# Wide one-hots, unscaled expert queries and fewer float32 pairs in a two-layer decoder trunk with a product-key FFN

## Chip, cores and metric

The kernel runs on one core of one Trainium2 chip. The metric is device time in microseconds of the whole program, the median over runs. The engines are named as in the profile: PE (TensorE, matrix multiplication), DVE (VectorE), ACT (ScalarE), POOL (GpSimd) and SP (SyncE, which issues the transfers). Every tensor in SBUF has 128 partitions.

## The reference, cut to what matters

There are two layers over 256 tokens of width 1024. A layer mixes tokens by three branches (sliding-window attention, a gated convolution and a recurrence), then applies the product-key FFN, then a gated projection of a side input. The change touches the FFN alone:

```
def peer(xn, w_q, sub_keys, u, v):          # t = 256 tokens, 8 heads, 128 x 128 keys, top 16
    q  = (xt @ w_q).reshape(t, 8, 2, 128)
    sc = einsum('thpc,pnc->thpn', q, sub_keys)
    top_s, top_i = top_k(sc, 16)
    cand = top_s[:, :, 0, :, None] + top_s[:, :, 1, None, :]
    best_s, best_c = top_k(cand.reshape(t, 8, 256), 16)
    i1, i2 = (take_along_axis(top_i[:, :, a], ...) for a in (0, 1))   # best_c // 16 and best_c % 16
    expert, gate = i1 * 128 + i2, softmax(best_s)
    act = gelu(einsum('cd,chkd->chk', x, u[expert]))
    return einsum('chk,chkd->cd', gate * act, v[expert])
```

Here xn = RMSNorm(h), that is h times a weight per column, times r2, one positive factor per token.

## The kernel before, in words

**All experts, densely.** The kernel doesn't gather rows of u and v. It multiplies the tokens by all 16,384 rows of u, weights the result with a matrix of gates that is zero where an expert wasn't chosen, and multiplies by all rows of v. Rows come in 64 *pairs* of 2 x 128 experts. `u_pass(i)` (line 642) loads one pair of u (1 MB), multiplies, and applies Gelu into a tile `acts` that holds four pairs. `v_pass(i)` (660) reads gates, multiplies them in, and accumulates into four PSUM banks. The loop at line 700 runs i from 0 to NPAIR + RUN_AHEAD: u_pass(i), and v_pass(i - RUN_AHEAD) once i has reached RUN_AHEAD.

**Two forms of a multiplication.** The result has to be nearly of float32 accuracy. Either PE multiplies in float32, or each operand is cut into a high and a low part (type float32r) and three products are summed (`mm3`, 184). For the second form `split` (153) makes the parts of 1024 columns of weights: ACT casts to the high part, DVE subtracts to get the low one. Each part has three buffers. In u_pass, pairs below WHOLE = 20 are multiplied in float32 straight from the loaded tile with the scaled tokens `x2w`; the others by mm3 with the parts of the scaled tokens `x2`. All other weights come through `Stream` (170), which splits the next 1024 columns as they are needed.

**Queries and routing.** For each of the eight heads `pair` multiplies the unscaled tokens `x2g` by the weights w_peer_q (two splits per head), DVE multiplies the result by r2 into `q` (507), and `scores` (485) multiplies by the keys and finds the top 16 of each half by DVE's instructions for maxima and their positions. `route(b)` (517) forms the candidates of 128 tokens, finds the best 16 and turns their positions into the two expert numbers e1 and e2; `soften(b)` (571) makes the gates gt with ACT's Exp; `turn(b)` (585) transposes e1, e2 and gt on PE and spreads each value over four neighbouring float16 elements (`eT`, and `g2` with high and low part).

**The matrix of gates.** For 8 tokens at a time, `hot(tg)` (601) compares eT with 0 to 127 and so makes one-hots on DVE: `o1` of e1 in a buffer of its own, `og` of e2, and two products of o1 with the parts of g2. `place(tg)` (620) has PE multiply these (16 multiplications of 128 x 128) into PSUM, ACT copies them to a stage, and every second group is written to HBM (`gd`). v_pass reads gd back. og is in pool `xp` with four buffers, two of which hold x2 during the FFN.

**What sets the order.** The framework fixes ahead of time an order for each engine's queue: of what is ready, what was written down first goes first, and instructions under `high_priority(offset=200)` (splits, loads and the queries' line 507) rank as if they had been written 200 instructions earlier. Each engine runs its queue in order. Tiles of one tag share that tag's buffers; route and turn share `rcode` (one buffer) and soften's gt shares one with route. By hand are written: scores of the last head and route(0) in pair 0; soften(0) ahead of pair 7; turn(0) and route(1) ahead of pair 8; soften(1) ahead of pair 13, turn(1) ahead of pair 14; and `matrix` (689), called three times in each pair: from pair G_START = 10 on, each call places the group before last and starts the one-hots of the next. There are 32 groups, so the last placing falls into pair 21. Line 713 demands that all of it was written down before v begins.

Of the kernel before, what the change touches and what calls it, by code (L numbers as in the profile page):

```python
# [7 lines left out]
F32 = mybir.dt.float32  # L8
F32R = mybir.dt.float32r
F16 = mybir.dt.float16  # L10
I32 = mybir.dt.int32
U32 = mybir.dt.uint32
AF = mybir.ActivationFunctionType
OP = mybir.AluOpType
# [4 lines left out]
P = 128  # L19
# [4 lines left out]
TOPK = 16  # L24
NPAIR = 64
G_START = 10
RUN_AHEAD = 24
WHOLE = 20
TG = 8
REP = 4  # L30
GPAD = 16
# [28 lines left out]
def plan():  # L60

    out = []

    def cols(name, c0, n):
        for c in range(n):
            for k in range(KT):
                out.append((name, k * P, c0 + c * P))

    cols("w_in", C_K, 2)
    cols("q", 0, 8)  # L70
    for k in range(KT):
        for m in range(2):
            out.append(("w_in", k * P, C_V + m * P))
    for j in range(0, KT, 2):
        cols("w_in", C_CX + j * P, 2)
        cols("w_in", C_CC + j * P, 2)
        cols("w_in", C_CB + j * P, 2)
    for j in range(0, KT, 2):
        cols("w_in", C_RX + j * P, 2)
        cols("w_in", C_RY + j * P, 2)  # L80
    for n in range(3):
        for j in range(0, KT, 2):
            cols("w_in", C_G + n * 1024 + j * P, 2)
            if n == 0:
                for name in ("w_rgate", "w_igate"):
                    for jo in range(2):
                        for ki in range(2):
                            out.append((name, (j // 2, ki * P), jo * P))
            cols("b%d" % n, j * P, 2)
    cols("w_out", 0, 8)  # L90
    cols("w_peer_q", 0, 16)
    for c in range(8):
        for k in range(2):
            out.append(("w_ple_proj", k * P, c * P))
    cols("w_ple_gate", 0, 8)
    return out
# [3 lines left out]
def trunk_kernel(ctx: ExitStack, tc: tile.TileContext, xT, pT, vecs, wmix, wu, wv, outT, dbg=None, layers=NL):  # L100
    nc = tc.nc
# [4 lines left out]
    xp = pool("xp", 4)  # L106
# [3 lines left out]
    small = pool("small", 2)  # L110
# [9 lines left out]
    def aux_bank(name, shape=(P, 2, T)):  # L120
        return psum.tile(list(shape), F32, name=name, tag="aux", bufs=2)
# [16 lines left out]
    ident = cst.tile([P, P], F32, name="ident")  # L138
# [11 lines left out]
    nc.gpsimd.memset(eps, EPS)  # L150


    def split(src, name, cuts=1):

        with tc.high_priority(offset=AHEAD):
            hi = parts.tile([P, 1024], F32R, name=name + "h", tag="hi")
            lo = parts.tile([P, 1024], F32R, name=name + "l", tag="lo")
            for c in range(cuts):
                s = slice(c * 1024 // cuts, (c + 1) * 1024 // cuts)
                nc.scalar.copy(hi[:, s], src[:, s])  # L160
                nc.vector.tensor_sub(lo[:, s], src[:, s], hi[:, s].bitcast(F32))
        return hi, lo

    def load(src, name):
# [5 lines left out]
    class Stream:  # L170
        def __init__(self, l):
            self.l, self.n, self.raw, self.cur = l, 0, None, None

        def next(self, w=1):
            if self.n % 16 == 0:
                self.raw = load(wmix[self.l, self.n // 16], "w%d_%d" % (self.l, self.n // 16)) if self.l or self.n else first
            if self.n % 8 == 0:
                o = self.n % 16 * P
                self.cur = split(self.raw[:, o : o + 1024], "w%d_%d" % (self.l, self.n // 8), 1 if self.l or self.n else 2)
            o = self.n % 8 * P  # L180
            self.n += w
            return self.cur[0][:, o : o + w * P], self.cur[1][:, o : o + w * P]
# [85 lines left out]
    def rb(rstd):  # L268
        return rstd[:, None, :].to_broadcast([P, 2, T])
# [12 lines left out]
    def t2(name, shape, dt=F32):  # L282
        return work.tile(list(shape), dt, name=name, tag="t2", bufs=3)
# [5 lines left out]
    def layer(l):  # L289
# [15 lines left out]
        for kt in range(KT):  # L305
            w = st.next(2)
# [196 lines left out]
        for hd in range(HEADS):  # L503
            ps = pair(st, x2g, L + "pq%d" % hd)
            q = work.tile([P, 2, T], F32, name=L + "pqs%d" % hd, tag="w2a")
            with tc.high_priority(offset=AHEAD):
                nc.vector.tensor_mul(q, ps, rb(r2))
            if last:
                scores(*last)
            last = (hd, q)  # L510
            if 2 <= hd < 6:
                x2 = scaled(V + V_FFN, r2, L + "n2", (2 * hd - 4, 2 * hd - 3), x2, x2w)
# [58 lines left out]
        def soften(b):  # L571
            n = L + "r%d" % b
            e1, e2, best = chosen[b]

            gt = small.tile([P, HEADS, TOPK], F32, name=n + "gt", tag="rsf", bufs=1)
            nc.vector.tensor_sub(gt, best, best[:, :, 0:1].to_broadcast([P, HEADS, TOPK]))
            nc.scalar.activation(gt, gt, AF.Exp)
            gs = small.tile([P, HEADS], F32, name=n + "gs", tag="rgs", bufs=1)
            nc.vector.tensor_reduce(gs, gt, axis=AX.X, op=OP.add)
            nc.vector.reciprocal(gs, gs)  # L580
            nc.vector.tensor_mul(gt, gt, gs[:, :, None].to_broadcast([P, HEADS, TOPK]))
            chosen[b] = (e1, e2, gt)


        def turn(b):
            n = L + "r%d" % b

            pt = aux_bank(n + "pt", (P, 3, P))
            for i, a in enumerate(chosen[b]):
                nc.tensor.transpose(pt[:, i, :], a.rearrange("p h k -> p (h k)"), ident)  # L590
            eT = small.tile([P, 2, P, REP], F16, name=n + "eT", tag="eT", bufs=2)
            nc.vector.tensor_copy(eT, pt[:, 0:2, :, None].to_broadcast([P, 2, P, REP]))
            g2 = small.tile([P, 2, P, REP], F16, name=n + "g2", tag="g2", bufs=2)
            rest = small.tile([P, P], F32, name=n + "rest", tag="rcode", bufs=1)
            nc.vector.tensor_scalar(rest, pt[:, 2, :], GS, None, op0=OP.mult)
            rep = rest[:, :, None].to_broadcast([P, P, REP])
            nc.vector.tensor_copy(g2[:, 0], rep)
            nc.vector.tensor_sub(g2[:, 1], rep, g2[:, 0])
            routed.append((eT, g2))

        def hot(tg):

            eT, g2 = routed[tg // (P // TG)]
            m = L + "t%d" % tg
            o = tg % (P // TG) * TG

            S = [P, TG, P // REP, REP]
            bc = lambda a: a[:, o : o + TG, None, :].to_broadcast(S)
            index = iota_i.rearrange("p (i r) -> p i r", r=REP)[:, None, :, :].to_broadcast(S)
            o1 = t2(m + "o1", S, F16)  # L610
            og = xp.tile([P, 3] + S[1:], F16, name=m + "og", tag="x")
            nc.vector.tensor_tensor(o1, index, bc(eT[:, 0, :]), op=OP.is_equal)
            nc.vector.tensor_tensor(og[:, 2], index, bc(eT[:, 1, :]), op=OP.is_equal)
            for i in range(2):
                nc.vector.tensor_mul(og[:, i], o1, bc(g2[:, i]))
            return og

        stage = [None]
# [195 lines left out]
```

## Time and profile before

| | |
|---|---|
| median of 3 runs | 2480.21 us (2479.56 to 2480.83) |
| the profiled execution's own time | 2482.27 us |
| its span on the core | 2480.6 us |
| granted TensorE clock, mean of the span | 0.991 |
| PE / DVE / ACT / POOL busy | 2443.6 / 1696.8 / 1228.9 / 28.8 us |
| moved by DMA | 485.92 MB, mean 196 GB/s |

The span is that of one profiled execution, and the time of that execution is 1.67 us longer. Busy times of different engines overlap, so they aren't added up. A granted clock of 1.00 is TensorE's full 2.4 GHz.

### The profile page before, as it was taken

Reading aid. Unit: us, or ns where it says so; the run is one execution under the profiler, and the core shown is the slowest. Engines: PE = TensorE matmul, PEld = TensorE weight load, DVE = VectorE, ACT = ScalarE, POOL = GpSimd, SP = SyncE. Lnnn points to the kernel's source line nnn. Section 1 sums busy time; section 2 is a strip of 40 time slices with the busy share of each in tenths; the row PEclk is TensorE's granted clock in tenths of the full one; section 3 lists DMA queues with packets and bytes.
Section 4 is the critical chain, followed back from the end, with each engine's and each line's share of the span. In section 5 each row is a group of like instructions: output and inputs, shape, how many; then the busy total and the mean of one; then the engine's idle time right before and its main releaser. Section 6 shows DMA issues by size and latency. Waiting matters only on the chain.

```text
span 2480.6 us, 40695 instructions
## 1 busy us (share of the span) xinstructions
PE 2443.6 (99%) x16696; PEld 2243.2 (90%) x16696; DVE 1696.8 (68%) x3020; ACT 1228.9 (50%) x1605; POOL 28.8 (1%) x44
## 2 busy tenths in 40 slices
PE   8999999999999999999999999999999999999997
PEld 7899999889999999988879999998899999999886
DVE  7666869987655555567776668699865555555666
ACT  5555544167444444444654564532664444444445
POOL 0000100000000000000000010000000000000000
PEclk9999999999999999999999999999999999999998
DMA  5255444468755656575424445533785565665752
GB/s 194 102 187 181 172 176 152 145 232 310 246 206 206 223 204 218 206 254 197 170 109 146 179 169 187 187 136 143 275 308 212 204 221 204 211 213 206 265 191 86
DMA packets 129452, 485.92 MB, mean 196 GB/s; under 512 B 7536, under 2 KB 73200, under 8 KB 74864
## 3 DMA queue, kind: packets, MB, share of 16 engines
q1 hardware_dynamic: 128976, 482.90, 54.8%
q8 instruction: 131, 2.15, 0.3%
q10 hardware_dynamic: 288, 0.41, 0.1%
q14 instruction: 57, 0.47, 0.1%
HBM read 448.67 MB, written 34.60 MB: 195 GB/s over the span
## 4 chain that ended last, share of the span: by engine, by line
PE 97%; DVE 2%; ACT 1%; DMA 1%; issue 0%; SPq 0%; DVEq 0%; ACTq 0%
PE L0acc L681 14%; PE L1acc L681 14%; PE L0ua L655 6%; PE L1ua L655 5%; PE L0ua L185 3%; PE L1ua L185 3%; PE L1ua L187 3%; PE L0ua L187 3%; PE L1ua L186 3%; PE L0ua L186 3%; PE L1mg L187 1%; PE L0mg L187 1%; PE L0mg L186 1%; PE L1mg L186 1%; PE L1mg L185 1%; PE L0mg L185 1%
## 5 line engine op out<-in xcount | busy, mean ns | idle before, releaser
L655 PE MATMUL L0ua<-L0n2w,L0u 128*128 128x256 f32 x640 | 145.1, 382 | 0.0
L655 PE MATMUL L1ua<-L1n2w,L1u 128*128 128x256 f32 x640 | 145.1, 382 | 0.0
L655 PEld LDWEIGHTS L1ua<-L1n2w,L1u 128*128 128x128 f32 x640 | 119.0, 190 | 14.8
L655 PEld LDWEIGHTS L0ua<-L0n2w,L0u 128*128 128x128 f32 x640 | 119.0, 190 | 14.8
L658 ACT ACTIVATE L1act<-L1ua 128x512 f32<-128x512 f32 x64 | 38.0, 594 | 46.4 <-PE L1ua L655 46.4
L658 ACT ACTIVATE L0act<-L0ua 128x512 f32<-128x512 f32 x64 | 38.0, 594 | 46.4 <-PE L0ua L655 46.3
L669 DVE TENSOR_TENSOR L0wt<-L0act,L0gr 128x256 f32<-128x256 f32 x128 | 53.4, 421 | 2.7 <-DMA L0gr<-L0gd 0.7
L669 DVE TENSOR_TENSOR L1wt<-L1act,L1gr 128x256 f32<-128x256 f32 x128 | 53.4, 421 | 2.5 <-DMA L1gr<-L1gd 0.5
L439 DVE RECIPROCAL L1ru<-L1ru 128x256 f32<-128x256 f32 x8 | 14.0, 1746 | 0.1
L439 DVE RECIPROCAL L0ru<-L0ru 128x256 f32<-128x256 f32 x8 | 13.9, 1743 | 0.1
L380 POOL MEMSET L1pc<- 128x4 f32 x4 | 0.4, 103 | 1108.1 <-DVE L1cy L388 1096.7
L367 PE MATMUL L0ao<-L0et,L0vt 128*64 128x512 f32 x24 | 12.4, 772 | 0.1
L362 PEld LDWEIGHTS L0at<-ident,L0e 128*128 128x128 f32 x48 | 6.6, 166 | 6.5 <-issue 2.1
L367 PE MATMUL L1ao<-L1et,L1vt 128*64 128x512 f32 x24 | 11.6, 696 | 0.1
L185 PE MATMUL L0k<-L0n1gh,w_0h 128*128 128x256 f32 x8 | 3.7, 457 | 7.4 <-ACT w_0h L160 7.2
L362 PEld LDWEIGHTS L1at<-ident,L1e 128*128 128x128 f32 x48 | 6.0, 153 | 5.3 <-DVE L1e L355 1.8
L409 DVE SCALAR_TENSOR_TENSOR L1xr<-L1pr,vec,L1xr 128x256 f32<-128x256 f32 x24 | 10.3, 481 | 0.0
L409 DVE SCALAR_TENSOR_TENSOR L0xr<-L0pr,vec,L0xr 128x256 f32<-128x256 f32 x24 | 10.3, 480 | 0.0
L362 PE MATMUL L0at<-ident,L0e 128*128 128x128 f32 x48 | 9.8, 332 | 0.0
L238 ACT CAST L1n2sh<-L1n2w 128x256 fp32r<-128x256 f32 x8 | 3.2, 406 | 13.2 <-DVE L1n2w L237 13.2
L364 ACT COPY L0et<-L0at 128x512 f32<-128x512 f32 x12 | 6.7, 580 | 6.3 <-PE L0at L362 6.3
L238 ACT CAST L0n2sh<-L0n2w 128x256 fp32r<-128x256 f32 x8 | 3.2, 406 | 13.2 <-DVE L0n2w L237 13.2
(6630 smaller groups left out, 9843.4 us busy)
## 6 DMA issues: line engine op xcount, KB each, us to landing
w<-wmix SPq DMA_DIRECT2D x137, 1024.0 KB, 4.8
L0u<-wu SPq DMA_DIRECT2D x64, 1024.0 KB, 4.9
L0v<-wv SPq DMA_DIRECT2D x64, 1024.0 KB, 4.8
L1u<-wu SPq DMA_DIRECT2D x64, 1024.0 KB, 4.8
L1v<-wv SPq DMA_DIRECT2D x64, 1024.0 KB, 4.8
L0gr<-L0gd SPq DMA_DIRECT2D x16, 1024.0 KB, 6.3
L1gr<-L1gd SPq DMA_DIRECT2D x16, 1024.0 KB, 5.9
L0gd<-L0t0st SPq DMA_DIRECT2D x1, 1024.0 KB, 3.8
```

What stands on the lines that cost most here:

```text
L185: nc.tensor.matmul(out, w[0], xh, start=start, stop=False, **kw)
L186: nc.tensor.matmul(out, w[0], xl, start=False, stop=False, **kw)
L187: nc.tensor.matmul(out, w[1], xh, start=False, stop=stop, **kw)
L362: nc.tensor.transpose(pt[:, g, :], ee[:, kv, g, kb * P : (kb + 1) * P], ident)
L364: nc.scalar.copy(et, pt)
L367: nc.tensor.matmul(po[kv * 64 : kv * 64 + 64, :, :], vt[:, kb, (2 * kt + kv) * 64 : (2 * kt + kv) * 64 + 64], ets[kv], start=kb == 0, stop ...
L409: nc.vector.scalar_tensor_tensor(o, pr[:, c, i : i + T], w[i], o, op0=OP.mult, op1=OP.add)
L439: nc.vector.reciprocal(u[:, c, :], u[:, c, :])
L655: nc.tensor.matmul(ps[:, e, :], raw[:, e * 1024 + kt * P : e * 1024 + kt * P + P], x2w[:, kt, :], start=kt == 0, stop=kt == KT - 1)
L658: nc.scalar.activation(acts[i // 4][:, i % 4 * 2 : i % 4 * 2 + 2, :], ps, AF.Gelu_apprx_tanh)
L669: nc.vector.tensor_mul(wt[:, e, :].rearrange("p (g t) -> p g t", t=SG), acts[i // 4][:, o + e, :].rearrange("p (g t) -> p g t", t=SG), gre ...
L681: nc.tensor.matmul(acc[b][c], wp[t[0]][:, e, b * P : (b + 1) * P], w[e][t[1]][:, c * 512 : (c + 1) * 512], start=i == 0 and e == 0 and t = ...
```

## The change

Five things are changed, all in the FFN.

- **Float32 pairs.** WHOLE goes from 20 to 8: pairs 8 to 19 of u are split and multiplied in three products.
- **Run-ahead.** RUN_AHEAD goes from 24 to 28: v_pass(0) follows u_pass(28).
- **Expert queries.** q is a copy by ACT of the product, without r2. As r2 is positive, the order of the scores stays; the factor enters in soften, where r2 of the 128 tokens is transposed on PE into a column `rc` which scales Exp's argument.
- **GpSimd low parts.** The low parts of w_peer_q (16 splits per layer) are subtracted by GpSimd.
- **One-hots.** eT and g2 are laid out so that e2 and e1, and the two parts of g2, lie side by side for each group of 8 tokens. One comparison over 2048 elements writes both one-hots into og, and one multiplication over 2048 elements writes both products. og has four planes in place of three, and o1 is gone.

```diff
-RUN_AHEAD = 24
-WHOLE = 20
+RUN_AHEAD = 28
+WHOLE = 8
...
-    def split(src, name, cuts=1):
+    def split(src, name, cuts=1, rest=nc.vector):
...
                 nc.scalar.copy(hi[:, s], src[:, s])
-                nc.vector.tensor_sub(lo[:, s], src[:, s], hi[:, s].bitcast(F32))
+                rest.tensor_sub(lo[:, s], src[:, s], hi[:, s].bitcast(F32))
...
-                self.cur = split(self.raw[:, o : o + 1024], "w%d_%d" % (self.l, self.n // 8), 1 if self.l or self.n else 2)
+                self.cur = split(self.raw[:, o : o + 1024], "w%d_%d" % (self.l, self.n // 8), 1 if self.l or self.n else 2,
+                                 nc.gpsimd if self.names[self.n] == "w_peer_q" else nc.vector)
...
             with tc.high_priority(offset=AHEAD):
-                nc.vector.tensor_mul(q, ps, rb(r2))
+                nc.scalar.copy(q, ps)
...
+            rt = aux_bank(n + "rt", (P, P))
+            nc.tensor.transpose(rt, r2[:, b * P : (b + 1) * P], ident)
+            rc = small.tile([P, 1], F32, name=n + "rc", tag="rrc", bufs=1)
+            nc.vector.tensor_copy(rc, rt[:, 0:1])
...
-            nc.scalar.activation(gt, gt, AF.Exp)
+            nc.scalar.activation(gt, gt, AF.Exp, scale=rc)
...
-            eT = small.tile([P, 2, P, REP], F16, name=n + "eT", tag="eT", bufs=2)
-            nc.vector.tensor_copy(eT, pt[:, 0:2, :, None].to_broadcast([P, 2, P, REP]))
-            g2 = small.tile([P, 2, P, REP], F16, name=n + "g2", tag="g2", bufs=2)
+            eT = small.tile([P, P // TG, 2, TG, REP], F16, name=n + "eT", tag="eT", bufs=2)
+            for i in range(2):
+                nc.vector.tensor_copy(eT[:, :, i], rep(pt[:, i, :]))
+            g2 = small.tile([P, P // TG, 2, TG, REP], F16, name=n + "g2", tag="g2", bufs=2)
...
-            o1 = t2(m + "o1", S, F16)
-            og = xp.tile([P, 3] + S[1:], F16, name=m + "og", tag="x")
-            nc.vector.tensor_tensor(o1, index, bc(eT[:, 0, :]), op=OP.is_equal)
-            nc.vector.tensor_tensor(og[:, 2], index, bc(eT[:, 1, :]), op=OP.is_equal)
-            for i in range(2):
-                nc.vector.tensor_mul(og[:, i], o1, bc(g2[:, i]))
+            og = xp.tile([P, 4, TG, P // REP, REP], F16, name=m + "og", tag="x")
+            flat = lambda a: a.rearrange("p a t i r -> p (a t) i r")
+            nc.vector.tensor_tensor(flat(og[:, 2:4]), index, bc(eT), op=OP.is_equal)
+            nc.vector.tensor_mul(
+                og[:, 0:2], og[:, 3:4].to_broadcast([P, 2, TG, P // REP, REP]), g2[:, o, :, :, None, :].to_broadcast([P, 2, TG, P // REP, REP]))
```

## Rows read from the trace of the kernel before

**Rows 1.** The page, busy time of each engine (share of the span, instructions).

```profile
PE 2443.6 (99%) x16696; PEld 2243.2 (90%) x16696; DVE 1696.8 (68%) x3020; ACT 1228.9 (50%) x1605; POOL 28.8 (1%) x44
```

**Rows 2.** PE's waits: total us, times, longest.

```profile
PE L0mg L187 <- DVE w_73l L161: 2.2, 1, 2.2
```

**Rows 3.** Stretches of layer 0: length, busy (instructions) by engine, clock, DMA share.

```profile
core 0: us, PE busy (x) PEld busy (x) DVE busy (x) ACT busy (x) POOL busy (x), PEclk, DMA share, GB/s
...
250.00:300.00 50.00, 47.79 (x386) 47.59 (x386) 44.21 (x49) 26.28 (x31) 8.50 (x5) 0.97 0.47 164
...
376.45:430.02 53.57, 53.57 (x447) 53.36 (x446) 51.30 (x195) 22.89 (x31) 0.00 (x0) 1.00 0.43 158
430.02:486.17 56.15, 56.15 (x267) 49.49 (x266) 52.94 (x283) 10.22 (x15) 0.00 (x0) 1.00 0.37 132
...
505.50:605.83 100.33, 100.33 (x852) 89.79 (x850) 82.62 (x128) 71.96 (x79) 0.00 (x0) 1.00 0.74 273
486.54:603.00 116.46, 116.46 (x911) 103.60 (x910) 100.24 (x153) 71.96 (x80) 0.00 (x0) 1.00 0.69 253
```

**Rows 4.** The chain that ended last, layer 0: start, us, work.

```profile
436.10 50.08 PE L0ua L655 x232
...
505.50 0.89 PE L0t0pg L630 x16
...
597.23 0.91 PE L0t28pg L630 x16
...
605.83 0.91 PE L0t31pg L630 x16
```

**Rows 5.** Timeline of ACT, two successive split pairs.

```profile
612.69 0.59 ACT L658 ACTIVATE L0act<-L0ua 128x512 f32<-128x512 f32 x1
...
618.45 0.60 ACT L658 ACTIVATE L0act<-L0ua 128x512 f32<-128x512 f32 x1
```

**Rows 6.** Timeline of DVE, layer 0.

```profile
260.05 2.29 DVE L161 TENSOR_TENSOR w_73l<-w,w_73h 128x1024 fp32r<-128x1024 f32 x1
...
387.54 1.22 DVE L161 TENSOR_TENSOR w_117l<-w,w_117h 128x1024 fp32r<-128x1024 f32 x1
...
446.57 0.27 DVE L524 TENSOR_TENSOR L0r0cand<-L0ts 128x128 f32<-128x128 f32 x1
...
486.54 1.23 DVE L592 CAST L0r0eT<-L0r0pt 128x1024 f16<-128x1024 f32 x1 [3.51 <-PE L0r0pt L590]
...
490.62 2.28 DVE L554 TENSOR_REDUCE L0r1code<-L0r1hit 128x128 f32<-128x2048 f32 x1
...
513.07 0.69 DVE L613 TENSOR_TENSOR L0t4og<-iota_i,L0r0eT 128x1024 f16<-128x1024 f16 x1 [0.49 <-PE L0t2pg L630]
...
584.99 1.23 DVE L161 TENSOR_TENSOR L0u200l<-L0u,L0u200h 128x1024 fp32r<-128x1024 f32 x1 [0.63 <-ACT L0u200h L160]
586.13 1.22 DVE L161 TENSOR_TENSOR L0u201l<-L0u,L0u201h 128x1024 fp32r<-128x1024 f32 x1
587.27 0.69 DVE L613 TENSOR_TENSOR L0t26og<-iota_i,L0r1eT 128x1024 f16<-128x1024 f16 x1
...
589.80 0.69 DVE L613 TENSOR_TENSOR L0t27og<-iota_i,L0r1eT 128x1024 f16<-128x1024 f16 x1
...
601.54 1.28 DVE L615 TENSOR_TENSOR L0t31og<-L0t31o,L0r1g 128x1024 f16<-128x1024 f16 x2
```

**Rows 7.** Groups by line and shape: busy us, mean ns.

```profile
L507 DVE TENSOR_TENSOR L0pqs<-L0pq,L0n2r 128x512 f32<-128x512 f32 x8 | 5.4, 678 | 0.0
```

**Rows 8.** Timeline of POOL, layer 0.

```profile
210.63 1.29 POOL L440 TENSOR_TENSOR L0ig<-L0ig,L0xr 128x512 f32<-128x512 f32 x1 [10.82 <-ACT L0ig L424]
...
256.57 6.90 POOL L441 TENSOR_TENSOR L0rc<-L0rc,L0ig 128x512 f32<-128x512 f32 x4 [1.69 <-issue]
```

**Rows 9.** Timeline of PE in the expert queries.

```profile
389.09 1.06 PE L489 MATMUL L0sc<-vec,L0pqs 128*128 128x128 f32 x8
...
392.85 0.28 PE L185 MATMUL L0pq<-L0n2gh,w_117h 128*128 128x256 f32 x1
...
395.74 1.06 PE L489 MATMUL L0sc<-vec,L0pqs 128*128 128x128 f32 x8
```

More of the change, by code (lines that the diff above doesn't have):

```diff
@@ L172, in __init__ @@
             self.l, self.n, self.raw, self.cur = l, 0, None, None
+            self.names = [name for name, _, _ in plan()]
         def next(self, w=1):
@@ L588, in turn @@
             pt = aux_bank(n + "pt", (P, 3, P))
-            for i, a in enumerate(chosen[b]):
+            e1, e2, gt = chosen[b]
+            for i, a in enumerate((e2, e1, gt)):
                 nc.tensor.transpose(pt[:, i, :], a.rearrange("p h k -> p (h k)"), ident)
-            eT = small.tile([P, 2, P, REP], F16, name=n + "eT", tag="eT", bufs=2)
-            nc.vector.tensor_copy(eT, pt[:, 0:2, :, None].to_broadcast([P, 2, P, REP]))
-            g2 = small.tile([P, 2, P, REP], F16, name=n + "g2", tag="g2", bufs=2)
+            G = [P, P // TG, TG, REP]
+            rep = lambda a: a.rearrange("p (g t) -> p g t", t=TG)[:, :, :, None].to_broadcast(G)
+            eT = small.tile([P, P // TG, 2, TG, REP], F16, name=n + "eT", tag="eT", bufs=2)
+            for i in range(2):
+                nc.vector.tensor_copy(eT[:, :, i], rep(pt[:, i, :]))
+            g2 = small.tile([P, P // TG, 2, TG, REP], F16, name=n + "g2", tag="g2", bufs=2)
             rest = small.tile([P, P], F32, name=n + "rest", tag="rcode", bufs=1)
             nc.vector.tensor_scalar(rest, pt[:, 2, :], GS, None, op0=OP.mult)
-            rep = rest[:, :, None].to_broadcast([P, P, REP])
-            nc.vector.tensor_copy(g2[:, 0], rep)
-            nc.vector.tensor_sub(g2[:, 1], rep, g2[:, 0])
+            nc.vector.tensor_copy(g2[:, :, 0], rep(rest))
+            nc.vector.tensor_sub(g2[:, :, 1], rep(rest), g2[:, :, 0])
             routed.append((eT, g2))
@@ L604, in hot @@
             m = L + "t%d" % tg
-            o = tg % (P // TG) * TG
-            S = [P, TG, P // REP, REP]
-            bc = lambda a: a[:, o : o + TG, None, :].to_broadcast(S)
+            o = tg % (P // TG)
+            S = [P, 2 * TG, P // REP, REP]
+            bc = lambda a: a[:, o].rearrange("p a t r -> p (a t) r")[:, :, None, :].to_broadcast(S)
             index = iota_i.rearrange("p (i r) -> p i r", r=REP)[:, None, :, :].to_broadcast(S)
-            o1 = t2(m + "o1", S, F16)
-            og = xp.tile([P, 3] + S[1:], F16, name=m + "og", tag="x")
-            nc.vector.tensor_tensor(o1, index, bc(eT[:, 0, :]), op=OP.is_equal)
-            nc.vector.tensor_tensor(og[:, 2], index, bc(eT[:, 1, :]), op=OP.is_equal)
-            for i in range(2):
-                nc.vector.tensor_mul(og[:, i], o1, bc(g2[:, i]))
+            og = xp.tile([P, 4, TG, P // REP, REP], F16, name=m + "og", tag="x")
[3 more added lines that the diff above has]
+                og[:, 0:2], og[:, 3:4].to_broadcast([P, 2, TG, P // REP, REP]), g2[:, o, :, :, None, :].to_broadcast([P, 2, TG, P // REP, REP]))
             return og
```

## Prediction

> **What bounds the kernel now.** I read the engine table of the page first: TensorE (PE) is busy 2443.6 us of a span of 2480.6 [rows 1]. The list of PE's waits is short; its longest entry in the body of a layer is 2.2 us [rows 2]. In the table by stage the reader is to see PE at 100% of its stage in the expert queries (376 to 430 us), in the first eight u pairs (430 to 486) and in the stretch with the one-hots (505.5 to 606), at a granted clock of 1.00, which is the 2.4 GHz level [rows 3]. So only a shorter PE program makes this kernel faster, and only while no other engine takes over. The one that can is VectorE (DVE): it is busy 52.94 of 56.15 us and then 100.24 of 116.46 us in those stretches, while ScalarE (ACT) has 71.96 of 100.33 [rows 3].
>
> **What leaves PE.** A float32 u pair is 32 PE instructions; 232 of them take 50.08 us [rows 4], so a pair takes 32 x 50.08 / 232 = 6.91 us. A split pair is 48 instructions; the Gelu copies of two successive split pairs start 612.69 and 618.45 us into the span, 5.76 us apart [rows 5]. Each of the pairs 8 to 19 saves 1.15 us of PE: 12 x 1.15 = 13.8 us per layer, 27.6 us in all. That is the ceiling.
>
> **What it costs DVE.** Each newly split pair gives ACT two casts and DVE two low parts. A low part lasts 1.23 us and follows its neighbour at 1.14 us [rows 6]; I count by such spacings. The one-hots before are four instructions per group; with no idle time between them the same step of two successive groups starts at 587.27 and 589.80, 2.53 us per group [rows 6]. A wide float16 instruction isn't in the trace. The float16 one of 1024 elements lasts 0.69 us [rows 6], as long as a float32 one of 512 (0.68) [rows 7], so I price 2048 in float16 as 1024 in float32: 1.14 us. Two make 2.28 us per group, 0.25 less, 8.0 us over 32 groups. The bounds are 2.53 (nothing saved) and, if the multiplication lost its double rate, 1.14 + 2.28 = 3.4 us, which would be 28 us per layer more; all operands keep their runs of four neighbouring elements, so I keep 2.28 and leave that end out of the range.
>
> **Where DVE can do it.** The relief in the query stage (16 low parts at 1.14 and 8 multiplications of 0.68 [rows 7], 24 us per layer) falls where nothing waits for it. Routing of the first half of the tokens starts at 446.57, after the scores of the last head; DVE then stands idle 3.51 us until the transposes of turn(0), which PE does at pair 8, bring it on at 486.54 [rows 6]. Pairs 0 to 7 stay float32, so PE reaches turn(0) no earlier. And the rest of route(1), from the sum at L554, can't come ahead of it: it shares single buffers with turn(0) (the tag rcode, and the tags of the expert numbers and of gt), and L554 runs at 490.62, after turn(0), though DVE had been idle [rows 6]. So the account opens at 486.54.
> - DVE, from there to the last one-hot, which ends at 602.8 [rows 6]: 100.24 us of work [rows 3]. Minus 8.0 for the one-hots. Plus 21 low parts (24 are needed, from the second of pair 9 to the first of pair 21, since three buffers are filled ahead; before there were 3) x 1.14 = 23.9. Plus 0.2 for the split copies of turn and the column of r2. Sum 116.3 us, so DVE ends at 602.8 at the earliest: where it ends now.
> - PE, same stretch: 2.75 pairs x 5.76 = 15.8 us up to the first placing, and then 10 1/3 pairs with three placings each. Before, PE starts those at 505.50; a split pair with its three placings takes 605.83 - 597.23 = 8.60 us [rows 4], so 88.9 us. Sum 104.7 us, 591.2.
>
> DVE owes 11.6 us more than PE. If PE followed the program's order strictly it would wait all of it at the placings and 2.2 us per layer would be left. It needn't: splits are queued 200 instructions ahead of their place, and a pair with placings issues about 115 (96 matmuls, 6 copies, 6 one-hots, 4 split parts, a Gelu, loads), so splits run 1.7 pairs ahead of the one-hots; a placing follows its one-hot by two calls, 0.67 pair. PE can thus be about 1.1 pairs of u ahead of the placings: 6.2 us of work, against 2.4 us more of low parts. What stays is 11.6 + 2.4 - 6.2 = 7.8 us, and about 2 us more for DVE waiting on casts and transposes (estimate: the idle times of 0.5 us ahead of a one-hot [rows 6], four of them). PE waits 9.8 us and keeps 13.8 - 9.8 = 4.0 us per layer: 8 us in all. Bounds: no run-ahead and 5 us of idle DVE, a loss of 2.8 per layer (+5.6); a run-ahead of three pairs or more, the whole 27.6.
>
> **What I cost at nothing.** Starting v at 28 moves no PE work: u and v pairs take the same PE time alone or together. It leaves 6.9 pairs between the last placing and the first v pass, which only matters if placings are late. The query copies on ACT (8, as long as a Gelu of the same size, 0.6 us [rows 5]) hide in a stage where ACT is busy 22.89 of 53.57 us [rows 3]. The two transposes of r2 per layer sit in the waits above; without that cover they are 0.2 us. Loads keep a 0.74 share of the DMA engines in the one-hot stretch [rows 3], whose length hardly changes. The clock stays at 1.00 in my sum: the slice with PE's 2.2 us wait has 0.97 [rows 3], so each longer gap would cost at most some 1.5 us, and I expect waits under a microsecond.
>
> **GpSimd low parts.** Sixteen per layer, 1024 elements, which the trace has not. A two-operand one of 512 took 1.29 us alone, and four in a row 6.90 us, 1.73 each, while DVE was subtracting [rows 8]; twice that is 2.6 to 3.5 us. PE goes from one head's scores to the next in 395.74 - 389.09 = 6.65 us [rows 9], 3.33 per split. A low part was ready at 388.76 and first used at 392.85 [rows 6, 9], 4.1 us of slack for the 1.4 to 2.3 us by which it gets longer. With 2.6 nothing is lost; with 3.5 it is (3.5 - 3.33) x 32 = 5.4 us. I take nothing, as DVE's subtractions and multiplications leave that very stage.
>
> While GpSimd multiplied, a DVE low part took 2.29 us in place of 1.23 [rows 6, 8]. The Trainium skill (GPSIMD Engine Reference, "8. Key points") says that GpSimd shares its SBUF interfaces with VectorE and contends with DVE instructions of two SBUF inputs; the trace agrees. By that rule what stays of such work on DVE in the query stage, the sixteen steps of the scaled x2, gets slower, and GpSimd goes to the upper bound: the sum by the rule is 5.4 us worse, which is the third rival. The same page ("3.1 Elementwise") gives 4497 ns for 2048 elements, half of which, 2.25 us, is an estimate under my lower bound; by it nothing is lost.
>
> **The rivals.**
> - PE stays the bound (chance 0.18). DVE's queue lets u run three or more pairs ahead, the placings go late, and the 6.9 pairs before v absorb them: from turn(0) to v, PE has 20 x 5.76 + 32 x 0.89 [rows 4] = 143.7 us of work, DVE 116.3 + 14 x 1.14 = 132.3. For it: a placing was split around u matmuls when its bank was late, so order does adapt. Against: low parts have the better rank only by 200 instructions. Gain 20 to 27.6 us: 2453 to 2460 us.
> - Slower by lockstep (0.18). Both wide instructions write into the one-hot's own buffer, of which there are two; before, the first wrote elsewhere and ran early. A one-hot of group k then can't begin until group k-2 is placed. DVE idles 0.49 us ahead of a one-hot for that already [rows 6]. It decides once PE finishes a placing later than DVE its one-hot; with 0.5 us on each of 30 groups the DVE account is 15 us longer, 13 us net of the 2 I put in: 26 us over two layers against my 8 gained, 2498 us; with half of it 2485.
> - GpSimd becomes the bound of the query stage (0.19): 3.5 us per low part, 5.4 us back, gain 2 to 3 us: 2478 us. From 3.6 us on it eats the gain. Against it: the single 1.29.
> - My forecast (0.45): DVE takes over as the bound from pair 10 on; gain 3 to 14 us, likeliest 8.
>
> **How the numbers follow.** The profiled execution took 2482.27 us, 1.67 more than its span and 2.06 above the median of 2480.21. The change of 8 us is taken off the median: 2472 us. The forecast's own range is 2466 to 2478. The 8-in-10 range reaches to the full gain (2452) and into the lockstep (2489). A difference under 0.2% (5 us) is about what this measurement can't tell from none. Faster: 0.33 of the forecast's 0.45, the first rival's 0.18, 0.01 of the third: 0.52. Same: 0.12 of the forecast, 0.02 of the second, 0.13 of the third: 0.27. Slower: 0.16 of the second, 0.05 of the third: 0.21.
>
> **What would show it.** One wide one-hot instruction near 1.22 us; DVE without idle time from turn(0) to the last one-hot, near 603 us in layer 0; PE's list of waits now with entries on og and on the low parts of u, some 10 us per layer, placings shifted against the u matmuls by about one pair; no PE wait on GpSimd. Wrong if the wide instructions take 2.2 us, if route(1)'s tail moves ahead of turn(0), if u leads the placings by three pairs, or if GpSimd's low parts take over 3.3 us.

## The result and the profile after

The changed kernel takes 2467.66 us (median of 5 runs, 2465.37 to 2469.17) against 2480.21 us (five runs as well): ratio 0.9946, 95% interval [0.9936, 0.9957], 12.5 us faster. The forecast was 2472 (its own range 2466 to 2478). Below "first product of v" and such are the starts of tiles on PE, read from the trace tile by tile.

The engine table of the changed kernel, which answers to [rows 1]:

```profile
PE 2417.5 (98%) x17084; PEld 2236.8 (91%) x17084; DVE 1715.4 (70%) x2900; ACT 1281.8 (52%) x1669; POOL 106.5 (4%) x76
```

PE lost 26 us of busy time. Only 22.8 us of it come from the stretches from the first u to the end of a layer (11.25 and 11.52), against a ceiling of 27.6; the rest comes from stretches that the change leaves alone. PE is no longer busy all through. The stretches of layer 0 that answer to [rows 3] (length, busy time of PE, weight loads, DVE, ACT, POOL, clock, DMA share):

```profile
376.00:430.00 54.00, 52.74 (x434) 52.09 (x434) 46.59 (x213) 26.99 (x41) 33.44 (x14) 1.00 0.44 156
430.00:486.00 56.00, 56.00 (x268) 49.36 (x267) 48.42 (x246) 10.98 (x16) 0.00 (x0) 1.00 0.41 150
486.00:640.00 154.00, 149.95 (x1489) 146.50 (x1489) 139.22 (x140) 117.56 (x131) 0.00 (x0) 1.00 0.75 266
```

PE stands idle 1.26 us in the queries and 4.05 us between 486 and 640; before it was idle in neither. Its longest waits there, with total, times and longest (they answer to [rows 2]; `st` is the stage into which ACT copies the placing banks):

```profile
PE L0pq L188 <- DVE L0n2gl L228: 1.0, 1, 1.0
...
PE L0t2pg L641 <- DVE L0t2og L625: 0.9, 1, 0.9
...
PE L0t3pg L641 <- ACT L0t2st L643: 0.7, 2, 0.4
...
PE L0t10pg L641 <- ACT L0t10st L643: 0.7, 1, 0.7
...
PE L0r1rt L579 <- ACT L0t6st L643: 0.6, 1, 0.6
```

Where the time came from, by first products on PE (us from the start of the span):

| stretch | before | after | difference |
|---|---|---|---|
| queries, layer 0: 376.5 to 429.9, after 374.1 to 429.2 | 53.4 | 55.1 | +1.7 |
| first u to the next layer: 429.9 to 1237.4, after 429.2 to 1229.5 | 807.5 | 800.3 | -7.2 |
| queries, layer 1: 1602.1 to 1655.5, after 1593.1 to 1648.2 | 53.4 | 55.1 | +1.7 |
| first u to the last projection: 1655.5 to 2429.6, after 1648.2 to 2412.7 | 774.1 | 764.5 | -9.6 |

The sum is -13.4 us. (The two profiled executions differ by 17.0 us of span; the rest lies ahead of these stretches, mostly in the attention, where the change does nothing.)

The timeline of DVE after (start, length, instruction, idle time before it) answers to [rows 6]:

```profile
485.85 1.23 DVE L161 TENSOR_TENSOR L0u90l<-L0u,L0u90h 128x1024 fp32r<-128x1024 f32 x1 [3.99 <-ACT L0u90h L160]
...
488.39 1.21 DVE L624 TENSOR_TENSOR L0t0og<-iota_i,L0r0eT 128x2048 f16<-128x2048 f16 x1
...
492.85 2.29 DVE L557 TENSOR_REDUCE L0r1code<-L0r1hit 128x128 f32<-128x2048 f32 x1
...
607.61 1.23 DVE L625 TENSOR_TENSOR L0t30og<-L0t30og,L0r1g 128x2048 f16<-128x2048 f16 x1
608.75 1.22 DVE L624 TENSOR_TENSOR L0t31og<-iota_i,L0r1eT 128x2048 f16<-128x2048 f16 x1
609.89 1.22 DVE L161 TENSOR_TENSOR L0u240l<-L0u,L0u240h 128x1024 fp32r<-128x1024 f32 x1
611.02 1.22 DVE L625 TENSOR_TENSOR L0t31og<-L0t31og,L0r1g 128x2048 f16<-128x2048 f16 x1
```

A wide one-hot instruction takes 1.22 us and follows its neighbour at 1.14, the price of the sum. The sum at L557 (L554 before) still stands behind turn(0). DVE works almost without a pause to 612.2, but the low part of u24 is done ahead of the last one-hot: at the last placing u is two and a half pairs ahead, not 1.1 (counted below). In the chain of waits of layer 0 the last placing comes at 612.45 (605.83 before [rows 4]); the first product of v starts at 644.2 (628.9 before).

### The profile page after: what moved, and what is told of

It reads as the page before. It is cut to its first block, busy times and chain, and to the rows that moved or that the text cites. A ratio compares the mean times of both kernels' runs of the same rounds, so it can differ in the third digit from the quotient of the medians.

```text
span 2463.6 us, 41520 instructions
## 1 busy us (share of the span) xinstructions
PE 2417.5 (98%) x17084; PEld 2236.8 (91%) x17084; DVE 1715.4 (70%) x2900; ACT 1281.8 (52%) x1669; POOL 106.5 (4%) x76
## 4 chain that ended last, share of the span: by engine, by line
PE 92%; DVE 4%; ACT 2%; issue 1%; DMA 0%; SPq 0%; DVEq 0%; ACTq 0%
PE L0acc L692 14%; PE L1acc L692 14%; PE L1ua L188 4%; PE L1ua L187 4%; PE L1ua L189 4%; PE L0ua L188 4%; PE L0ua L187 4%; PE L0ua L189 4%; PE L1ua L666 2%; PE L0ua L666 2%; PE L0mg L189 1%; PE L0mg L187 1%; PE L0mg L188 1%; PE L0y L189 1%; PE L0y L187 1%
## 5 line engine op out<-in xcount | busy, mean ns | idle before, releaser
L666 PE MATMUL L0ua<-L0n2w,L0u 128*128 128x256 f32 x256 | 55.7, 379 | 0.0
L666 PE MATMUL L1ua<-L1n2w,L1u 128*128 128x256 f32 x256 | 55.7, 379 | 0.0
L666 PEld LDWEIGHTS L1ua<-L1n2w,L1u 128*128 128x128 f32 x256 | 48.4, 190 | 6.5
L666 PEld LDWEIGHTS L0ua<-L0n2w,L0u 128*128 128x128 f32 x256 | 48.4, 190 | 6.5
L497 DVE MAX8 L1ts<-L1scs 128x8 f32<-128x128 f32 x32 | 7.6, 280 | 5.5 <-ACT L1scs L493 5.5
L497 DVE MAX8 L0ts<-L0scs 128x8 f32<-128x128 f32 x32 | 7.6, 280 | 5.4 <-ACT L0scs L493 5.4
```

The lines of the kernel that those rows point to most:

```text
L497: nc.vector.max(v[:, 0:8], s)
L666: nc.tensor.matmul(ps[:, e, :], raw[:, e * 1024 + kt * P : e * 1024 + kt * P + P], x2w[:, kt, :], start=kt == 0, stop=kt == KT - 1)
```

## The experiments

All ratios are to the kernel before on the same chip, beside 0.9946 [0.9936, 0.9957] of the changed kernel. "Per layer" compares first u to the end of the layer, layer 0 and layer 1, with the 800.3 and 764.5 us of the changed kernel.

**Low parts of the queries back on DVE.**

```diff
-                                 nc.gpsimd if self.names[self.n] == "w_peer_q" else nc.vector)
+                                 nc.vector)
```

> The changed kernel with the low parts of the query weights back on DVE; the query copies stay on ACT. Theory (DVE's account opens at turn(0), so relief in the query stage is worth nothing, and GpSimd there only holds up DVE's norm): PE's 1.3 us of waiting at the first query products of each layer goes, nothing is lost elsewhere; 2.5 to 3.5 us faster than the changed kernel, some 2464.5 us. Rival (the relief is needed, because DVE would still be at scores and routing when turn(0) comes): slower than the changed kernel by 2 to 5 us per layer, 2472 to 2478 us.

Measured: 2465.38 us, ratio 0.9939 [0.9926, 0.9952]. The total differs from the changed kernel's by less than the measurement tells, but the trace shows the place: both query stages take 53.4 us again, and PE's waits at their head are gone. From the first u on nothing moves (800.6 and 764.5). The cost of GpSimd, 1.7 us per layer, is shown. How it arises is in the changed kernel's timelines of POOL and DVE just ahead of the queries:

```profile
369.63 2.41 POOL L161 TENSOR_TENSOR w_112l<-w,w_112h 128x1024 fp32r<-128x1024 f32 x1 [108.45 <-ACT w_112h L160]
372.52 2.47 POOL L161 TENSOR_TENSOR w_113l<-w,w_113h 128x1024 fp32r<-128x1024 f32 x1 [0.48 <-ACT w_113h L160]
```

```profile
365.76 0.68 DVE L209 TENSOR_TENSOR L0n2sq<-L0n2sq,L0n2s 128x512 f32<-128x512 f32 x1
...
369.99 2.72 DVE L228 SCALAR_TENSOR_TENSOR L0n2gl<-h,vec,L0n2gh 128x256 fp32r<-128x256 f32 x2 [0.73 <-ACT L0n2gh L227]
372.64 2.89 DVE L209 TENSOR_TENSOR L0n2sq<-L0n2sq,L0n2s 128x512 f32<-128x512 f32 x1
```

The same DVE instruction takes 0.68 us without GpSimd and 2.89 beside a low part that GpSimd begins at 372.52. GpSimd's own low parts take 2.37 to 2.60 us in this layer. DVE is what waits, in the normalization that the first products of the queries need.

**Twenty float32 pairs again, all else changed.**

```diff
-WHOLE = 8
+WHOLE = 20
```

> The changed kernel with 20 float32 pairs as before; all its other parts stay. Theory: PE is then the bound from the first u pair to v as in the kernel before, so wide one-hots and relieved DVE bring nothing, and GpSimd costs 1.7 us per layer in the query stage; 2483 us (2480 to 2485). Rival (the other parts bring time of their own): under 2478 us.

Measured: 2484.84 us, ratio 1.0013 [1.0005, 1.0022], as expected: the wide one-hots, the unscaled queries and the run-ahead of 28 buy nothing without the pairs, and GpSimd's part remains.

**The pairs alone.** The kernel before with the two constants of the change.

```diff
-RUN_AHEAD = 24
-WHOLE = 20
+RUN_AHEAD = 28
+WHOLE = 8
```

> The kernel before with 8 float32 pairs and a run-ahead of 28, nothing else: narrow one-hots, low parts and scaling of the queries on DVE. Theory: PE has no loss in the query stage (3.4 us better than the changed kernel), and DVE has 8 us more one-hot work per layer after turn(0), of which PE loses 3 to 8 us as u's lead absorbs the rest; 2471 to 2480 us. Rival (the relief of DVE in the query stage carries the gain): no gain or a loss, 2481 us or more.

Measured: 2478.82 us, ratio 0.9995 [0.9986, 1.0003]: nothing, the upper edge of what was expected. In layer 0, 500 to 600, PE is busy 90.20 us of 100 and DVE 96.97. Neither these two constants nor the rest of the change gains by itself; together they gain 12.5 us.

**Run-ahead back to 24.**

```diff
-RUN_AHEAD = 28
+RUN_AHEAD = 24
```

> The changed kernel with v 24 pairs behind u as before. Theory: the last placing comes at 612 us while u is at pair 24, so the first v pass must be late for its gates, but PE's queue is ordered by what is ready and takes further u pairs instead; within 2 us of the changed kernel, 2466 to 2470 us. Rival (the four pairs are needed: PE waits for write and read back of the gates after the last placing): 5 to 10 us more per layer, 2477 to 2488 us.

Measured: 2481.06 us, ratio 1.0006 [0.9997, 1.0016]. The theory, which was the prediction's, fell: the four pairs are worth 13 us. The chain of waits of this run:

```profile
610.25 0.51 PE L0t31pg L641 x8
610.78 0.49 ACT L0t30st L643
611.28 0.40 issue
611.67 1.10 ACT L0t30st L643
612.79 7.42 DMA L0gd<-L0t30st
620.34 7.44 DMA L0gr<-L0gd
627.81 0.77 DVE L0wt L680 x2
628.60 0.63 ACT L0wp0h L275
629.27 5.76 PE L0acc L692 x24
```

From the last placing to the first product of v the gates go out to DRAM (7.42 us) and come back (7.44): 19 us in all, 3.3 pairs of u. Each engine's queue holds its instructions in an order that is fixed when the program is built; with 24 PE runs 857 - 750 = 107 split products of u between the two in layer 0, 12.8 us at 0.12 each, and with 28 it runs 1008 - 750 = 258, 31 us (first products of v and of the last group, by their place among the split products of u in the trace). Between 620 and 640 this run's PE is busy 16.67 us of 20. Before, the last placing was 23 us ahead of the first v (605.83 and 628.9) and the same number was enough.

**turn(0) a pair earlier.**

```diff
-G_START = 10
+G_START = 9
```

> The changed kernel with G_START 9 in place of 10: turn(0), which PE reached at pair 8, comes at pair 7, one float32 pair (6.91 us) earlier; no work is added or taken away. Theory (from turn(0) on DVE is the bound, to its last one-hot at 612.2, and PE loses 4.05 us per layer by it): DVE had 7.6 us idle between 430 and 486, so the account opens up to 6.9 us earlier, the last one-hot ends near 606, PE's waits in the stretch with the one-hots vanish, about 2460 us (2457 to 2464). Rival (DVE's idle time before turn(0) is needed by the end of routing, or the first low parts are what PE waits for): the same time as the changed kernel, 2467.7 within 2.

Measured: 2470.36 us, ratio 0.9963 [0.995, 0.9977]. The last placing did come 6.2 us earlier after the first u (176.9 us behind it, 183.1 in the changed kernel), but PE was idle 5.26 us between 486 and 640 and not less. The theory that DVE's end, 612.2, costs PE its time fell: the end came earlier and PE's waits stayed.

**Buffers of their own for the routings**, so that route(1) needn't wait for turn(0).

```diff
-... tag="r" + (tag or name), bufs=1)
+... tag="r" + (tag or name) + (str(b) if name in ("e1", "e2", "sf") else ""), bufs=1)
-            gt = small.tile(..., tag="rsf", bufs=1)
+            gt = small.tile(..., tag="rsf%d" % b, bufs=1)
-            rest = small.tile(..., tag="rcode", bufs=1)
+            rest = small.tile(..., tag="rrest", bufs=1)
```

> The changed kernel with buffers of their own for the two routings (e1, e2, sf and gt twice, rest apart from code), so that the tail of route(1) from L554 on, 9.7 us, needn't stand behind turn(0). Nothing else changes. Theory (these shared buffers put the tail behind turn(0), and DVE's account from there decides): L554 of route(1) starts before turn(0)'s casts at 487, DVE's idle 4 us ahead of them is filled, the last one-hot ends some 4 us earlier, PE's waits halve, 2463.5 us (2460 to 2466). Rival (DVE reaches the tail only then anyway): L554 stays near 492.9 and the time at 2467.7 within 2.

Measured: 2477.57 us, ratio 0.9989 [0.998, 0.9998]. The sum moved to 474.01, as the prediction's reading of the shared buffers says, but now it stands ahead of soften(0), and turn(0) waits. PE's list of waits and the stretches around it:

```profile
PE L0r0pt L598 <- DVE L0r0gt L588: 4.2, 1, 4.2
```

```profile
484.00:486.00 2.00, 0.00 (x0) 0.00 (x0) 2.00 (x3) 1.41 (x3) 0.00 (x0) 1.00 0.39 49
486.00:488.00 2.00, 0.38 (x2) 0.38 (x3) 1.97 (x6) 1.81 (x2) 0.00 (x0) 0.55 0.83 340
488.00:490.00 2.00, 2.00 (x11) 2.00 (x11) 2.00 (x4) 0.00 (x0) 0.00 (x0) 0.50 0.98 414
490.00:492.00 2.00, 2.00 (x12) 2.00 (x11) 2.00 (x4) 0.00 (x0) 0.00 (x0) 0.50 0.58 246
492.00:494.00 2.00, 2.00 (x15) 2.00 (x15) 0.70 (x1) 0.90 (x1) 0.00 (x0) 0.74 0.00 0
```

The wait of 4.2 us also costs the clock: the grant falls during it and is 0.50, the 1.2 GHz level, until about 493.

**The rank of the splits of u**, 100 and 300 instructions in place of 200 (the same edit with either number; `split` takes it as an argument).

```diff
-                    w = split(raw[:, e * 1024 : (e + 1) * 1024], L + "u%d%d" % (i, e))
+                    w = split(raw[:, e * 1024 : (e + 1) * 1024], L + "u%d%d" % (i, e), ahead=100)
```

> The changed kernel with the splits of the u pairs queued 100 instructions ahead of their place in place of 200. Theory (the lead of u over the placings is set by that rank; behind the last placings a pair issues only some 57 instructions, so 200 were 2.9 pairs there): the lead at the last placing falls to 0.4 pairs, 2.5 pairs x 5.76 = 14 us less of PE work in front of it, DVE has 5 low parts less (5.7 us) before its last one-hot, which ends near 606.5; PE waits some 8 us more per layer, 2483 us (2476 to 2487). Rival (the three buffers of the parts, not the rank, limit the lead): the time stays at 2467.7 within 2 and u24's low part is still done before the last one-hot.

> The changed kernel with the splits of the u pairs queued 300 instructions ahead of their place in place of 200. Theory (the rank sets the lead): u leads by 1.7 pairs more at the last placing, PE's waits among the one-hots fall from 4.05 us to under 1 per layer, DVE's last one-hot ends 3 to 4 us later, near 616; the gate's way through DRAM from the last placing to the first product of v, 18 us, then ends near 634, when PE still has u to do: about 2463 us (2459 to 2467). Rival A (three buffers limit the lead already): as the changed kernel, 2467.7 within 1.5. Rival B (the later placings make the first v pass late, as with RUN_AHEAD 24): 2470 to 2476.

Measured: 2473.96 us, ratio 0.9968 [0.9956, 0.9981], with 100; 2470.73, ratio 0.9959 [0.9946, 0.9973], with 300. A lower rank costs some 5 us, not 15, and in the profiled execution a part of that comes through the clock (last section); a higher one gains nothing. The lead of u can be counted in PE's order: split products of u that the trace has ahead of the first product of a group, layer 0 (48 are a pair; the program's own text has 198, 390, 516, 582 and 630). The counts in the last expectation below are nine higher each, which changes no difference between them.

| group | 4 | 16 | 24 | 28 | 31 |
|---|---|---|---|---|---|
| changed kernel | 251 | 481 | 630 | 700 | 750 |
| rank 100 | 239 | 433 | 582 | 652 | 702 |
| rank 300 | 262 | 492 | 632 | 712 | 753 |
| pairs alone (above) | 238 | 448 | 569 | 640 | 721 |
| narrow (below) | 240 | 448 | 569 | 640 | 721 |
| narrow, rank 300 (below) | 249 | 492 | 619 | 712 | 774 |

In the changed kernel u leads by (251 - 198) / 48 = 1.1 pairs at group 4, (481 - 390) / 48 = 1.9 at group 16 and (750 - 630) / 48 = 2.5 at the last. From group 16 on rank 100 takes one pair of it, not 2.5; rank 300 adds next to none.

**Twelve float32 pairs.**

```diff
-WHOLE = 8
+WHOLE = 12
```

> The changed kernel with 12 pairs of u in float32 in place of 8: PE gets back 4 x 1.15 = 4.6 us per layer of work, DVE loses 8 low parts and ACT 8 casts, just where the first placings fall. Theory (PE's 4 us of idle time per layer come from DVE and ACT being behind among the first dozen placings, 505 to 550, not from DVE's total): that idle time goes to under 1.5 us, net 1 to 2 us per layer: ratio to the kernel before 0.9955 to 0.9962, against 0.9946 of the changed kernel. Rival (the idle time has nothing to do with the split pairs there): 9.2 us more, ratio 0.998.

Measured: 2477.21 us, ratio 0.9994 [0.9985, 1.0003]; 804.8 and 770.0 us per layer, 4.5 and 5.5 more, about the 4.6 us by which four pairs are longer. PE is still idle 3.3 us between 486 and 640. The rival was right: of the 4.05 us of idle time the eight extra low parts among the first placings account for 0.75 at most.

**Own buffers and a turn(0) one pair later.** The edit of the own buffers, and:

```diff
-G_START = 10
+G_START = 11
```

> The routing buffers of the run before with their own tags, and G_START 11: turn(0) at pair 9, so DVE has the time of a whole pair to finish the tail of route(1) ahead of turn(0), and the one-hots start 5.8 us later. Theory (what PE loses is the tail of route(1), 9.7 us, lying among the first one-hots; the run-ahead of 28 has some 14 us to spare, as the last placing at 612.3 and the first product of v at 644.2 are 32 us apart and the way through DRAM takes 18): PE no longer stalls at turn(0), its idle time from 486 to 640 falls from 4.05 us to about 1, ratio 0.991 to 0.9935. Rival (ACT's copies of the banks are what is short, with or without the tail): idle time stays at 3 to 5 us, ratio 0.9945 to 0.996. Third (the later placings delay v, as with RUN_AHEAD 24): ratio over 0.997.

Measured: 2469.41 us, ratio 0.9958 [0.9945, 0.9972]. The stall at turn(0) is gone, PE is idle 3.5 us from 486 to 640, and the time is that of the changed kernel. The sum stands at 476.02, ahead of turn(0), so it isn't the tail of route(1) that PE waits for. As the one-hots also start a pair later here, the two effects aren't measured apart.

**Narrow one-hots in the new layout.**

```diff
-            nc.vector.tensor_tensor(flat(og[:, 2:4]), index, bc(eT), op=OP.is_equal)
-            nc.vector.tensor_mul(og[:, 0:2], og[:, 3:4].to_broadcast(...), g2[...].to_broadcast(...))
+            for i in (1, 0):
+                nc.vector.tensor_tensor(og[:, 2 + i], index, bc(eT[:, o, i]), op=OP.is_equal)
+            for i in range(2):
+                nc.vector.tensor_mul(og[:, i], og[:, 3], bc(g2[:, o, i]))
```

> The changed kernel with each of the two wide one-hot instructions cut in two of 1024 elements, in the same buffer and layout. By the rows of before four take 2.53 us per group, the two wide ones 2.28: 8.0 us more DVE per layer. Theory (DVE paces the placings, and the lead of u and the run-ahead swallow most of that): last placing 6 to 8 us later, near 619; PE loses 1 to 3 us per layer more: ratio 0.9955 to 0.9975. Rival (the width is what made the change a gain, as the pairs alone brought nothing): 5 us per layer and more, ratio over 0.9985. Null (the layout and the unscaled queries did it, not the width): ratio 0.9946 within 0.0008.

Measured: 2489.66 us, ratio 1.0035 [1.0021, 1.0049]: in this layout the width is worth some 22 us, more than the whole gain, though it saves DVE little. The timelines of DVE, first of the narrow run:

```profile
567.06 1.31 DVE L624 TENSOR_TENSOR L0t18og<-iota_i,L0r1eT 128x1024 f16<-128x1024 f16 x2
568.26 1.32 DVE L626 TENSOR_TENSOR L0t18og<-L0t18og,L0r1g 128x1024 f16<-128x1024 f16 x2
569.47 1.25 DVE L161 TENSOR_TENSOR L0u180l<-L0u,L0u180h 128x1024 fp32r<-128x1024 f32 x1
570.60 1.32 DVE L624 TENSOR_TENSOR L0t19og<-iota_i,L0r1eT 128x1024 f16<-128x1024 f16 x2
```

and of the changed kernel:

```profile
566.27 1.22 DVE L624 TENSOR_TENSOR L0t18og<-iota_i,L0r1eT 128x2048 f16<-128x2048 f16 x1
567.40 1.22 DVE L161 TENSOR_TENSOR L0u190l<-L0u,L0u190h 128x1024 fp32r<-128x1024 f32 x1
568.54 1.22 DVE L625 TENSOR_TENSOR L0t18og<-L0t18og,L0r1g 128x2048 f16<-128x2048 f16 x1
569.68 1.22 DVE L624 TENSOR_TENSOR L0t19og<-iota_i,L0r1eT 128x2048 f16<-128x2048 f16 x1
```

Four narrow instructions take 569.47 - 567.06 = 2.41 us, two wide ones 2 x 1.14 = 2.28: 4.2 us of DVE per layer. But beside group 18 the one run makes the low part of u18, the other that of u19. The eight groups from 16 to 24 take 26.0 and 25.9 us, alike; in them PE runs 569 - 448 = 121 split products in the narrow run and 630 - 481 = 149 in the changed one, at 0.12 us each 3.4 us more work in the same time. The stretches from 580 to 600, first of the narrow run, then of the changed kernel, show the same: DVE nearly full in both, PE idle 1.88 us and 0.28.

```profile
580.00:600.00 20.00, 18.12 (x194) 17.21 (x193) 19.12 (x29) 16.33 (x19) 0.00 (x0) 1.00 0.70 262
```

```profile
580.00:600.00 20.00, 19.72 (x216) 19.06 (x216) 19.70 (x18) 17.30 (x20) 0.00 (x0) 1.00 0.74 268
```

What PE waits for is something else again. Of the narrow run's 11.66 us of idle time from 486 to 640 its list of waits puts 9.5 us down to ACT's copies of the placing banks and 0.7 to one-hots (2.9 and 0.9 of 4.05 in the changed kernel); two of the entries:

```profile
PE L0r1pt L598 <- ACT L0t8st L643: 1.3, 1, 1.3
...
PE L0t17pg L641 <- ACT L0t16st L643: 0.7, 1, 0.7
```

How fewer u products between the placings and a full DVE become waits for ACT is not shown. Nor are all 22 us due to width as such. The pairs alone, with the narrow one-hots of before and from group 16 on the same counts in the table above, took 808.3 and 773.4 us per layer, against 812.2 and 775.3 here and 800.3 and 764.5 with wide ones. In the one-hots of before o1 has a buffer of its own; here all four instructions write into the one-hot's two buffers, and DVE waits 2.4 us for them in layer 0.

**The narrow one-hots with rank 300** for the splits of u (both edits above).

> The narrow one-hots of the last run with the splits of u queued 300 instructions ahead in place of 200. The work is the same instruction for instruction; only the order in which the queues hold it changes: the first product of group 16 then stands behind 501 split products of u in PE's queue and that of group 31 behind 783, against 457 and 730 of the narrow run and 490 and 759 of the changed kernel. Theory (what the width buys is mostly that the order of the build lets u run ahead of the placings; with u ahead PE has work while DVE paces the placings): PE's idle time from 486 to 640 falls from 11.7 us to 4 to 6, ratio 0.995 to 0.999, last placing later than the 617.9 of the narrow run. Rival (DVE's time for the narrow instructions is lost whatever the order): idle time over 9 us and ratio over 1.001.

Measured: 2482.46 us, ratio 1.001 [1.0002, 1.0019]. From 486 to 640 PE is idle 8.65 us, against 11.66 of the narrow run and 4.05 of the changed kernel; per layer it takes 808.3 and 772.6 us, against 812.2 and 775.3. Neither theory: the order alone, with the same instructions, gives back 6 of the 22 us (1.0035 to 1.001). In the middle this queue has little more than the narrow one (619 - 492 = 127 products from group 16 to 24), and DVE again waits 2.4 us for the one-hot's own two buffers:

```profile
567.75 1.29 DVE L624 TENSOR_TENSOR L0t17og<-iota_i,L0r1eT 128x1024 f16<-128x1024 f16 x2 [0.78 <-PE L0t15pg L641]
...
577.89 1.29 DVE L624 TENSOR_TENSOR L0t20og<-iota_i,L0r1eT 128x1024 f16<-128x1024 f16 x2 [0.56 <-PE L0t18pg L641]
```

## Why the prediction came out

The direction and the size were right, within 5 us, and so was the way in which PE keeps a part of its 13.8 us per layer: u runs ahead of the placings while DVE is full. But several terms of the sum were off and partly cancelled, so that the time fell into the forecast's own range is in part luck. The forecast's mechanism, that DVE takes over as the bound, did not come out as stated: PE is busy 149.95 of 154 us, and DVE's end 6.2 us earlier brought nothing. Of its signs, the 10 us of PE waits on one-hots and low parts of u are missing; most of the idle time stands against ACT's copies. What held is nearer to the first rival ("PE stays the bound"), whose 20 to 27.6 us were too much.

- **The ceiling, the wide one-hots, the relief of the query stage, turn(0).** Right. The price of 1.14 us held. Without the fewer float32 pairs the rest is worth nothing (1.0013), and turn(0)'s casts start at 487.00 (486.54 before).
- **DVE's account.** Sized too small. It gave 602.8 at the earliest; DVE's last one-hot ended at 612.2. The account stopped at the first low part of pair 21, and two more were added for the lead of 1.1 pairs; DVE went on to the first of pair 24, six more than in the account, 6.8 us. The third low part that was to stand ready ahead of turn(0) came only at 485.85, as the load of u9 was late (ACT's cast of it waited 3.79 us for the load), and ran ahead of turn(0)'s casts, 1.1 us more. The first u came 0.7 us earlier than before. That makes 610.0; DVE's idle time from 485.85 to 612.25, 2.3 us, is the rest.
- **The run-ahead of u: the step that was mis-sized.** The prediction took one lead of 1.1 pairs for all placings, and so a wait of 9.8 us per layer. The lead was 1.1 pairs at group 4, as taken, but grew to 1.9 at group 16 and 2.5 at the last; PE was idle 4.05 and 3.14 us, and 7.2 and 9.6 us per layer stayed. The count by rank was the wrong model: half the rank took one pair away and half as much again gave nothing. What the lead buys was right in kind: from 580 to 600 DVE is nearly full and PE hardly idle, which is the first rival's mechanism ("the placings go late, and the 6.9 pairs before v absorb them"). The number there is a pair short: from the last placing to v the program's own text has 1008 - 630 = 378 products, 7.9 pairs, and from turn(0) to v 21 pairs, not 20.
- **"Starting v at 28 moves no PE work."** True as worded, and its condition, late placings, was met; but it was costed at nothing where it is worth 13 us. With 24 the gates' way through DRAM isn't covered by work of PE.
- **GpSimd at nothing.** Off by 1.7 us per layer. The prediction watched GpSimd's own length (2.6 to 3.5; it was 2.37 to 2.60) and took its slack from it. The cost came through DVE. The Trainium skill (GPSIMD Engine Reference, "8. Key points") has the contention; the trace agrees (0.68 to 2.89 us), but here it is DVE's instructions that are held. The estimate of 2.25 us from the Trainium skill (GPSIMD Engine Reference, "3.1 Elementwise") lies a little under the 2.37 to 2.60 measured.
- **Lockstep on og's two buffers.** Not in the changed kernel. In both narrow runs the waits it names are there, 2.4 us in layer 0 of each, so it was a fair rival.

Of the 13.8 us per layer 6.6 and 4.2 are missing. Idle time is 4.05 of the first; the rest are delays too short to count as idle. The profile shows a split product as 0.283 us long (the end is modelled) and the next one starts 0.12 later, so a delay of up to 0.16 us stays hidden. By the starts of PE's instructions from the first u to the first v of layer 0, the 35 changes from a u product to a placing take 7.73 us, where 0.122 each would be 4.27; the steps inside the placings take 28.79, against 26.96 before; and the two changes to the transposes of the second half of the tokens 1.32 in place of 0.24. These 6.4 us are nearly all that is missing. In layer 1 the same count gives 5.4, and there the kernel before already lost 1.5.

Open: PE's 3 to 5 us of idle time per layer stayed with an earlier or later turn(0), with the tail of route(1) out of the way and with fewer splits; much of it stands in waits for ACT's copies of the placing banks, but no run took a copy away. And the 16 us that the narrow run still lacks with rank 300 aren't divided between DVE's 4.2 us per layer, the waits for og, ACT's copies and the order.

The lowest median of the kernels tried is that of the change with the low parts of the queries on DVE: 2465.38 us, 0.9939 [0.9926, 0.9952], not clear of the change itself in total.

## What to carry to other kernels

When an engine off the path becomes full, ask what the queues' order lets the bounding engine do meanwhile: with narrow one-hots a larger lead of u in PE's queue, and nothing else, took PE's idle time in layer 0 from 11.7 to 8.7 us, and such a lead can be counted from the order of the queue. A lead only helps if what comes behind is equally late: the run-ahead must cover the late placings plus their way through DRAM. And parts that gain nothing alone (1.0013 and 0.9995) may gain together, so a part's worth is read with the others in place. Last, a busy share can hide short delays, here 2.3 of 6.4 us; the starts of the instructions show them.

## What was not expected of the hardware

A two-operand GpSimd low part of 1024 elements took 2.47 us, as others did (2.37 to 2.60), while a DVE instruction of 0.68 us beside it took 2.89. That GpSimd never loses by it isn't shown: before, four of its instructions in a row took 1.73 us each while DVE subtracted, and one alone 1.29 [rows 8]. In the run with own buffers PE stood still for 4.2 us; the granted clock fell to 0.50 in that time and stayed there for some 5 us after. Behind the idle times of up to a microsecond in the changed kernel's layer 0 it stayed at 1.00 from 486 to 640. The run with rank 100 has a second such place, in layer 1, where PE was busy 2.64, 2.76 and 2.87 us of 4 each before and while the grant fell. The 0.57 of two stretches is a mean over both levels; from 1769 to 1775 the grant is 0.50:

```profile
1760.00:1764.00 4.00, 2.64 (x28) 2.20 (x27) 2.68 (x5) 4.00 (x6) 0.00 (x0) 1.00 0.47 199
1764.00:1768.00 4.00, 2.76 (x28) 2.43 (x29) 4.00 (x6) 3.19 (x4) 0.00 (x0) 1.00 0.64 262
1768.00:1772.00 4.00, 2.87 (x26) 2.75 (x24) 4.00 (x6) 2.56 (x3) 0.00 (x0) 0.57 0.02 4
1772.00:1776.00 4.00, 4.00 (x24) 3.96 (x23) 3.34 (x3) 0.65 (x2) 0.00 (x0) 0.57 0.71 266
```
